# Long convolution: one tile of three as diagonal matmuls, the other two accumulated in PSUM, and row scalings read from PSUM

## Chip, cores and metric

The kernel runs on one core of a Trainium2 chip. The metric is the device time of one execution in microseconds; the time of a kernel is the median of its runs.

## What is computed

A two-block network over 512 positions of width 1024 (batch 1, float32 throughout). The change concerns the first stage of the first block, the three mixers:

```python
a = rmsnorm(h, g_mix)
z = a @ w_in                                    # 1024 -> 2304 columns
za, zb, zc = z[..., :768], z[..., 768:1536], z[..., 1536:]
# A: y = val * sigmoid(gate); causal depthwise convolution of width 31 over 384 channels, + bias;
#    layernorm in groups of 64 channels; silu
ya = conformer_conv(za, conv_a_w, conv_a_b, ln_a_g, ln_a_b)
# B: bg * (causal depthwise convolution of width 3 of cg * xb), 256 channels
yb = short_gated_conv(zb, conv_b_w)
# C: u * (ws @ layernorm(v) + b), a mix over blocks of 128 positions, 384 channels
yc = spatial_gating(zc, ln_c_g, ln_c_b, w_s, b_s)
h = h + concatenate([ya, yb, yc]) @ w_out
```

Behind it come a large expert layer (the product of all 16384 experts, with routing), a gated embedding, and the second block; all of that is left as it is.

## The kernel before

**Layout.** Activations are held transposed: a tile has 128 channels on the partitions and the 512 positions along the free dimension. The 384 channels of the long convolution are three tiles; `conv_a_w` gives each channel 31 weights, which stand as columns in one constant tile (`self.col`).

**Products.** A float32 product is made of three products in the format fp32r: a tensor x is split into `h`, its value cast to that format, and `l = x - h`. `mm3` (L233 to L235) issues h·wh, l·wh and h·wl into one PSUM accumulation. Weights come by DMA into `raw` (SyncE's queue, L202), ScalarE casts them to `wh` (L216), and GpSimd subtracts to get `wl` (L217). Activations are split by `split` (ScalarE, L227; VectorE, L228). `proj` makes one 128x512 output tile from eight such weight units (24 matmuls) in one of four PSUM buffers named `mm`. Two PSUM buffers are named `sm` and two `gg`.

**The stage in program order** (`mix`). The first four column tiles are multiplied while x is still being loaded; `rs` is the reciprocal root mean square of each position, spread over all partitions, and each projection is scaled by it when it leaves PSUM. Then: gate and value of the three tiles of A, which give `yp` (30 zeros and 512 values of y); the first tap of each convolution on ScalarE (L503); the 384 columns of v for C (`vt`), their layernorm; the three `uz` of C; `short(0)`; `short(1)` with `spatial` (48 small matmuls) inside; the remaining 30 taps of each of the three tiles (L590), each one VectorE instruction `ca = yp[:, k : k + 512] * w[k] + ca`; `group_ln` of all three tiles. `group_ln` is a generator: `proj_out` runs one of its steps after each of the eight full-width products of the output projection with the inputs that are ready first (`ys`), and then makes two half-width passes with the late inputs (`late`). At the end of each half the next layer's normalization starts.

**Order.** The order of instructions on each engine is fixed when the program is built. A planner simulates the engines with a cost model and gives each engine, of what is ready in the simulation, what comes first in program order. So the taps, last in program order, fill VectorE's free time. On the chip each engine then works its list in order and waits by semaphores.

**Buffers that matter.** `yq`, the padded input of the short convolution, has one buffer: GpSimd clears its first two columns (L549) for `short(1)` after VectorE has read it for `short(0)` (L555, L557). GpSimd also does the scaling of `g` (L493), of `uz` (L540) and of the six inputs of `short` (L484), the product `yq` (L550), the last product of `short` (L558), and the bias and gate of `spatial` (L576, L577). For these ScalarE first copies the tile out of PSUM.

Of the kernel before, what the change touches and what calls it, by code (L numbers as in the profile page):

```python
# [10 lines left out]
F32 = mybir.dt.float32  # L11
F32R = mybir.dt.float32r
# [4 lines left out]
AF = mybir.ActivationFunctionType  # L17
ALU = mybir.AluOpType
# [4 lines left out]
P = 128  # L23
S = 512
NT = S // P
# [99 lines left out]
def run(gen):  # L125
    for _ in gen:
        pass
# [12 lines left out]
class Net:  # L140
# [166 lines left out]
            self.nc.tensor.matmul(ss[:, t : t + 1], sq[t * P // HS][:, c], self.ones, start=True, stop=True)  # L307
        return ss

    def rsqrt(self, ss, dim, w=NT):  # L310

        ms = self.small(w, tag="ms")
        self.nc.vector.tensor_scalar(ms, ss[:, :w], SQ / dim, SQ * EPS, ALU.mult, ALU.add)
        return self.inv_sqrt(ms, w)

    def inv_sqrt(self, ms, w):

        v = self.nc.vector
        y, a, b = (self.small(w, tag=t, bufs=n) for t, n in (("ry", 4), ("ra", 2), ("rb", 2)))
        yi = y.bitcast(I32)  # L320
        v.tensor_scalar(yi, ms.bitcast(I32), 1, None, ALU.logical_shift_right)
        v.tensor_scalar(yi, yi, -1.0, float(0x5F3759DF), ALU.mult, ALU.add)
        v.tensor_tensor(a, y, y, ALU.mult)
        v.tensor_tensor(a, a, ms, ALU.mult)
        v.scalar_tensor_tensor(b, a, -10.0 / 3, a, ALU.add, ALU.mult)
        v.scalar_tensor_tensor(y, b, 5.0, y, ALU.add, ALU.mult)
        v.tensor_tensor(a, y, y, ALU.mult)
        v.scalar_tensor_tensor(a, a, -0.5 / SQ, ms, ALU.mult, ALU.mult)
        v.scalar_tensor_tensor(y, a, 1.5, y, ALU.add, ALU.mult)
        return y  # L330
# [66 lines left out]
        return xs  # L397


    def group_ln(self, ys, lng, lnb, func, out):  # L400

        nc = self.nc
        blk = self.col("blk", 0, 2)
        w = 2 * NT

        def stats(tiles):
            ss = self.psm()
            for c, y in enumerate(tiles):
                for t in range(NT):
                    o = c * w + 2 * t  # L410
                    nc.tensor.matmul(ss[:, o : o + 2], y[:, t * P : (t + 1) * P], blk, start=True, stop=True)
            return ss

        n = len(ys) * w
        rows = lambda r: [self.heads_rows(r[:, c * w : (c + 1) * w]) for c in range(len(ys))]
        m = self.small(n, tag="lm")
        nc.vector.tensor_scalar(m, stats(ys)[:, :n], 1.0 / 64, None, ALU.mult)
        es = rows(m)
        yield
        yc, q = [], []  # L420
        for c, y in enumerate(ys):
            mb = self.turned(es[c])
            yc.append(self.g(name="yc"))
            nc.vector.tensor_tensor(yc[c], y, mb, ALU.subtract)
            q.append(self.g(name="sq"))
            nc.scalar.activation(q[c], yc[c], AF.Square)
        yield
        yield
        es = rows(self.rsqrt(stats(q), 64, n))
        yield  # L430
        yield
        for c in range(len(ys)):
            rb = self.turned(es[c])
            o = self.g(name="ln")
            nc.vector.scalar_tensor_tensor(o, yc[c], self.col(lng, c), rb, ALU.mult, ALU.mult)
            nc.scalar.activation(o, o, func, bias=self.col(lnb, c))
            out(o)

    def mixers(self, X, then=None):
# [7 lines left out]
    def mix(self, X, mx):  # L447
        nc = self.nc
# [12 lines left out]
        rs = self.e("rs", 1)  # L461
# [4 lines left out]
        bs = mx.tile([P, 3, P], F32, tag="bs", name="bs")  # L466
# [5 lines left out]
        def prod():  # L472
            nonlocal u
            if first:
                return first.pop(0)
            u += KD
            return self.proj(st, u - KD, xs)

        def z(tag, bufs, pool=False):
            p = prod()  # L480
            o = self.e(tag, bufs)
            if pool:
                nc.scalar.copy(o, p)
                nc.gpsimd.tensor_tensor(o, o, rs, ALU.mult)  # L484
            else:
                nc.vector.tensor_tensor(o, p, rs, ALU.mult)
            return o

        yp = []
        for c in range(3):  # L490
            g = z("za", 3)
            nc.scalar.activation(g, g, AF.Sigmoid)
            nc.gpsimd.tensor_tensor(g, g, rs, ALU.mult)  # L493
            y = mx.tile([P, 30 + S], F32, tag="yp", name=self.nm("yp"), bufs=3)
            nc.gpsimd.memset(y[:, :30], 0.0)
            nc.vector.tensor_tensor(y[:, 30:], prod(), g, ALU.mult)
            yp.append(y)
        ya = []
        for c in range(3):
            a = self.e("ca", 3)  # L500
            w = lambda k, c=c: self.col("conv_a_w", 31 * c + k)
            tap = lambda k, c=c: yp[c][:, k : k + S]
            nc.scalar.activation(a, tap(0), AF.Identity, bias=self.col("conv_a_b", c), scale=w(0))  # L503
            ya.append((a, w, tap))
        w1 = self.psm()
        for c in range(3):
            for h in range(2):
# [15 lines left out]
                    self.mm3(vp[t], (xs[k][0][:, sl], xs[k][1][:, sl]), st.unit(u + 3 * k, 3), k == 0, k == KD - 1)  # L523
        u += 3 * KD
        for t, p in enumerate(vp):
            v = mx.tile([P, 384], F32, tag="vt", name=self.nm("vt"), bufs=NT)
            nc.scalar.activation(v, p, AF.Copy, scale=rc[:, t : t + 1])
            m = self.small(6, tag="vm")
            nc.vector.tensor_reduce(m, h6(v), AX.X, ALU.add)
            nc.vector.tensor_scalar(m, m, -1.0 / 64, None, ALU.mult)  # L530
            nc.vector.tensor_tensor(h6(v), h6(v), m[:, :, None].to_broadcast([P, 6, 64]), ALU.add)
            q = self.g(name="sq")
            nc.scalar.activation(q[:, :384], v, AF.Square)
            nc.vector.tensor_reduce(var[:, 6 * t : 6 * t + 6], h6(q[:, :384]), AX.X, ALU.add)
            vt.append(v)
        uz = []
        for c in range(3):
            uz.append(self.e("zu", 3))
            nc.scalar.copy(uz[c], prod())
            nc.gpsimd.tensor_tensor(uz[c], uz[c], rs, ALU.mult)  # L540
        r = self.rsqrt(var, 64, 6 * NT)
        for t in range(NT):
            rb = r[:, 6 * t : 6 * t + 6, None].to_broadcast([P, 6, 64])
            nc.vector.tensor_tensor(h6(vt[t]), h6(vt[t]), rb, ALU.mult)

        def short(c, between=lambda: None):
            cg, xb = z("zb", 4, True), z("zb", 4, True)
            y = mx.tile([P, 2 + S], F32, tag="yq", name=self.nm("yq"), bufs=1)
            nc.gpsimd.memset(y[:, :2], 0.0)  # L549
            nc.gpsimd.tensor_tensor(y[:, 2:], cg, xb, ALU.mult)  # L550
            between()
            bg = z("zb", 4, True)
            a = self.e("cb", 2)
            w = lambda k: self.col("conv_b_w", 3 * c + k)
            nc.vector.tensor_scalar(a, y[:, 0:S], w(0), None, ALU.mult)  # L555
            for k in range(1, 3):
                nc.vector.scalar_tensor_tensor(a, y[:, k : k + S], w(k), a, ALU.mult, ALU.add)  # L557
            nc.gpsimd.tensor_tensor(a, a, bg, ALU.mult)  # L558
            return a

        sg = []
# [1 line left out]
        def spatial():  # L563
            for c in range(3):
                mp = self.psm()
                for h in range(2):
                    for t in range(NT):
                        nc.tensor.matmul(
                            mp[64 * h : 64 * h + 64, t * P : (t + 1) * P],
                            vt[t][:, c * P + 64 * h : c * P + 64 * h + 64], wsT[:, 2 * c + h, :],  # L570
                            start=True, stop=True,
                        )
                o = self.e("sg", 3)
                nc.scalar.activation(o, mp, AF.Copy, scale=self.col("ln_c_g", c))
                o3 = o.rearrange("p (t i) -> p t i", t=NT)
                nc.gpsimd.tensor_tensor(o3, o3, bs[:, c, None, :].to_broadcast([P, NT, P]), ALU.add)  # L576
                nc.gpsimd.tensor_tensor(o, o, uz[c], ALU.mult)  # L577
                sg.append(o)

        free = [(("za", 3), ("za", 3)), (("zu", 3), ("zu", 3)), (("zb", 4), ("zb", 4)), (("zb", 4), ("zb", 4))]  # L580
        late = []
        out = lambda o: late.append(self.split(o, tags=free[len(late)]))
        ys = [self.split(short(0))]
        b1 = short(1, spatial)
        ys += [self.split(o) for o in (sg[0], sg[1], b1)]
        out(sg[2])
        done = []
        for a, w, tap in ya:
            for k in range(1, 31):
                nc.vector.scalar_tensor_tensor(a, tap(k), w(k), a, ALU.mult, ALU.add)  # L590
            done.append(a)
        return ys, late, self.group_ln(done, "ln_a_g", "ln_a_b", AF.Silu, out)


    def peer_norm(self, X):
# [1093 lines left out]
```

## Time and profile before

| what | value |
|---|---|
| median of 3 runs | 3199.23 us (3198.02 to 3207.88) |
| the profiled execution | 3196.37 us, span 3194.6 us, mean granted TensorE clock 0.977 |
| TensorE (PE) busy | 3048.8 us, 95% of the span, 15428 matmuls |
| VectorE (DVE) busy | 1905.5 us, 60% |
| ScalarE (ACT) busy | 1049.6 us, 33% |
| GpSimd (POOL) busy | 1465.6 us, 46% |
| DMA | 424.88 MB, mean 133 GB/s |

The profile is of one execution. Its span runs from the first to the last instruction; the execution is 1.8 us longer. PEld is TensorE's loading of weights, which overlaps its matmuls. Matmuls are pipelined and their ends are modelled, so the distance between the starts of two tells their cost, not the duration shown. The granted clock is given as a share of full speed: 1.0 is 2.4 GHz, 0.5 is 1.2 GHz. A time line gives the start, the duration, the instruction as "out<-in" with tile names, the count where several were merged, and in brackets the idle time before and what ended it.

### The profile page before, as it was taken

How to read it: one execution, taken by the hardware profiler on the slowest of the kernel's cores; microseconds unless marked ns; L12 is line 12 of the kernel's file. 1: busy time of each engine (PE TensorE's matmuls, PEld its weight loads, DVE VectorE, ACT ScalarE, POOL GpSimd, SP SyncE). 2: the span in 40 equal slices, each digit the busy share in tenths (PEclk: the TensorE clock that was granted, in tenths of full speed). 3: DMA queues.
4: the chain of work that ended last, by engine and by line, in shares of the span. 5: the costliest groups of instructions: out<-in, count | busy, mean ns of one | idle time of the engine just before them, and what ended most of it. 6: DMA issues, size and time to landing. Idle time of an engine off the chain costs nothing.

```text
span 3194.6 us, 38906 instructions
## 1 busy us (share of the span) xinstructions
PE 3048.8 (95%) x15428; PEld 2545.1 (80%) x15428; DVE 1905.5 (60%) x3262; ACT 1049.6 (33%) x1632; POOL 1465.6 (46%) x777
## 2 busy tenths in 40 slices
PE   8589999999999999999999988899999999999998
PEld 7478888777878888888888877778888887888887
DVE  8964778988667676676555566666211277552123
ACT  4232222444422322222222344343322234432222
POOL 5635666333345444454444443533444431234454
PEclk9889999999999999999999989999999999999999
DMA  3222333565775656665555311112222221122321
GB/s 135 73 79 93 119 119 139 198 237 208 264 247 197 211 199 207 214 224 193 202 188 177 109 67 60 53 41 79 89 91 105 99 76 38 53 92 76 116 88 65
DMA packets 131926, 424.88 MB, mean 133 GB/s; under 512 B 7824, under 2 KB 73872, under 8 KB 97184
## 3 DMA queue, kind: packets, MB, share of 16 engines
q1 hardware_dynamic: 131744, 422.40, 37.5%
q8 instruction: 121, 1.98, 0.3%
q14 instruction: 61, 0.50, 0.1%
HBM read 367.84 MB, written 54.53 MB: 132 GB/s over the span
## 4 chain that ended last, share of the span: by engine, by line
PE 47%; DVE 5%; issue 1%; ACT 1%; POOL 1%; DVEq 0%; POOLq 0%; ACTq 0%
PE mm L233 15%; PE mm L234 15%; PE mm L235 15%; DVE l L380 1%; PE sm L1239 1%; PE sm L1203 1%; DVE sq L297 0%; DVE m L371 0%; PE gg L1266 0%; PE sm L307 0%; PE gg L1260 0%; DVE x L980 0%; PE mm L1395 0%; PE sm L337 0%; POOL wl L217 0%
## 5 line engine op out<-in xcount | busy, mean ns | idle before, releaser
L217 POOL TENSOR_TENSOR wl<-raw,wh 128x1024 fp32r<-128x1024 f32 (+4 forms) x526 | 1280.2, 2456 | 1544.5 <-ACT wh L216 1537.2
L233 PE MATMUL mm<-h,wh 128*128 128x512 f32 (+1 forms) x2524 | 962.0, 382 | 24.3 <-DVE x L980 7.5
L235 PE MATMUL mm<-h,wl 128*128 128x512 f32 (+1 forms) x2524 | 951.6, 378 | 23.0 <-POOL wl L217 22.9
L234 PE MATMUL mm<-l,wh 128*128 128x512 f32 (+1 forms) x2428 | 924.9, 381 | 16.8 <-DVE l L228 12.4
L216 ACT CAST wh<-raw 128x1024 fp32r<-128x1024 f32 (+4 forms) x526 | 510.1, 996 | 938.1 <-issue 524.1
L235 PEld LDWEIGHTS mm<-h,wl 128*128 128x128 f32 x2524 | 482.0, 191 | 112.7 <-POOL wl L217 26.7
L233 PEld LDWEIGHTS mm<-h,wh 128*128 128x128 f32 x2524 | 482.5, 191 | 111.5 <-DVE x L980 8.7
L234 PEld LDWEIGHTS mm<-l,wh 128*128 128x128 f32 x2428 | 464.6, 191 | 100.6 <-DVE l L228 13.0
L233 PE MATMUL mm<-ah,wh 128*128 128x512 f32 x1024 | 399.3, 390 | 5.3 <-DVE x L640 5.3
L234 PE MATMUL mm<-al,wh 128*128 128x512 f32 x1024 | 399.1, 390 | 0.0
L235 PE MATMUL mm<-ah,wl 128*128 128x512 f32 x1024 | 399.0, 390 | 0.0
L942 DVE CUSTOM_DVE_ANT_0 aw<-aw,c 128x1024 f32<-128x1024 f32 x96 | 199.6, 2081 | 118.0 <-DMA aw<-in_ada_w 94.8
L640 DVE TENSOR_TENSOR x<-x,mm 128x512 f32<-128x512 f32 x256 | 172.6, 681 | 144.5 <-PE mm L235 144.5
L233 PEld LDWEIGHTS mm<-ah,wh 128*128 128x128 f32 x1024 | 192.6, 188 | 46.8 <-DVE x L640 4.4
L234 PEld LDWEIGHTS mm<-al,wh 128*128 128x128 f32 x1024 | 192.5, 188 | 40.1
L235 PEld LDWEIGHTS mm<-ah,wl 128*128 128x128 f32 x1024 | 192.6, 188 | 40.0
L1488 DVE TENSOR_TENSOR sg<-sg,mm 128x512 f32<-128x512 f32 (+1 forms) x48 | 30.9, 643 | 301.4 <-PE mm L235 288.0
L629 ACT CAST ah<-a 128x512 fp32r<-128x512 f32 x128 | 79.4, 621 | 333.8 <-DVE a L627 202.2
L980 DVE SCALAR_TENSOR_TENSOR x<-mm,mod,x 128x256 f32<-128x256 f32 (+1 forms) x112 | 66.5, 595 | 188.5 <-PE mm L235 188.4
L627 DVE TENSOR_TENSOR a<-a,g 128x512 f32<-128x512 f32 x128 | 139.8, 1118 | 61.6 <-DMA a<-act_d 47.4
L630 DVE TENSOR_TENSOR al<-a,ah 128x512 fp32r<-128x512 f32 x128 | 141.2, 1109 | 40.7 <-ACT ah L629 39.5
L233 PE MATMUL mm<-g,wh 128*128 128x512 f32 (+1 forms) x416 | 148.6, 357 | 0.0
(391 smaller groups left out, 3789.4 us busy)
## 6 DMA issues: line engine op xcount, KB each, us to landing
raw<-in_expert_u SPq DMA_DIRECT2D x64, 1024.0 KB, 5.3
raw<-in_expert_v SPq DMA_DIRECT2D x64, 1024.0 KB, 5.1
aw<-in_ada_w SPq DMA_DIRECT2D x96, 512.0 KB, 4.6
raw<-in_ffn_w_in SPq DMA_DIRECT2D x44, 1024.0 KB, 4.8
g_d<-gs SPq DMA_DIRECT2D x16, 2048.0 KB, 7.9
g<-g_d SPq DMA_DIRECT2D x32, 1024.0 KB, 6.3
act_d<-a SPq DMA_DIRECT2D x18, 1024.0 KB, 3.9
a<-act_d SPq DMA_DIRECT2D x18, 1024.0 KB, 4.8
```

What stands on the lines that cost most here:

```text
L216: self.keep(nc.scalar.copy(h[:, c], raw[:, c]))
L217: nc.gpsimd.tensor_tensor(lo[:, c], raw[:, c], h[:, c].bitcast(F32), ALU.subtract)
L233: nc.tensor.matmul(out, w[0], x[0], start=start, stop=False)
L234: nc.tensor.matmul(out, w[0], x[1], start=False, stop=False)
L235: nc.tensor.matmul(out, w[1], x[0], start=False, stop=stop)
L380: nc.vector.scalar_tensor_tensor(lo[:, c], t, sh(k), h[:, c].bitcast(F32), ALU.add, ALU.subtract)
L627: nc.vector.tensor_tensor(v3(a), v3(a), g4[:, :, j, :], ALU.mult)
L629: nc.scalar.copy(h, a)
L630: nc.vector.tensor_tensor(lo, a, h.bitcast(F32), ALU.subtract)
L640: nc.vector.tensor_tensor(X[n], X[n], p, ALU.add)
L942: nc.vector.tensor_tensor_reduce(w, w, c, 1.0, 0.0, ALU.mult, ALU.add, self.mod[:, i : i + 1])
L980: self.nc.vector.scalar_tensor_tensor(x, p, self.mod[:, o + n : o + n + 1], x, ALU.mult, ALU.add)
```

## The change

- Two of the three convolution tiles accumulate their taps in PSUM (`gg`) instead of SBUF; only the last tap writes `ca` in SBUF. Their 60 taps are traced at fixed places between the other work (`tap(n)`), instead of at the end.
- The third tile goes to TensorE: `yp` is split into `yh` and `yl`, the 31 weights into `wh` and `wl`; for each tap ScalarE makes two 128x128 diagonal matrices (`dh`, `dl`: the identity scaled by a column of weights; six buffers each), and `mm3` multiplies them with the shifted `yh`, `yl`, all 31 taps into one PSUM tile. ScalarE adds the bias when it copies it out.
- `group_ln` is called twice: for the first two tiles, its steps between the diagonal products, and for the third, its steps in `proj_out` as before.
- Row scalings (`g`, `uz`, the inputs of `short`) are VectorE instructions that read the projection from PSUM. `cg` is scaled by `rs2`, the square of `rs`, and `xb` is not scaled or stored by itself: `y = xb * cg` reads it from PSUM. `short`'s other products and the two steps of `spatial` are VectorE's too, those of `spatial` reading PSUM. GpSimd keeps the clearing of paddings and the weight splits.
- `spatial` comes after `short(1)`, no longer inside it. The new parameters `room` (the width of a small buffer) and `c0` (the number of the first tile) let `group_ln` work on part of the tiles.

```diff
+    def rsqrt(self, ss, dim, w=NT, room=None):
...
-    def group_ln(self, ys, lng, lnb, func, out):
+    def group_ln(self, ys, c0, lng, lnb, func, out):
...
-        def z(tag, bufs, pool=False):
-            p = prod()
+        def z(tag, bufs, scale=None):
             o = self.e(tag, bufs)
-            if pool:
-                nc.scalar.copy(o, p)
-                nc.gpsimd.tensor_tensor(o, o, rs, ALU.mult)
-            else:
-                nc.vector.tensor_tensor(o, p, rs, ALU.mult)
+            nc.vector.tensor_tensor(o, prod(), rs if scale is None else scale, ALU.mult)
             return o
+        def taps():
+            for c in range(2):
+                acc = self.ps("gg", 2)
+                nc.scalar.activation(acc, tap(0), AF.Identity, bias=self.col("conv_a_b", c), scale=w(0))
+                for k in range(1, 31):
+                    if k == 30:
+                        done.append(self.e("ca", 3))
+                    o = done[c] if k == 30 else acc
+                    nc.vector.scalar_tensor_tensor(o, tap(k), w(k), acc, ALU.mult, ALU.add)
+                    yield
...
+        gated(0)
+        gated(1)
+        nc.vector.tensor_tensor(rs2, rs, rs, ALU.mult)
+        tap(12)
+        gated(2)
+        nc.scalar.copy(yh, yp[2])
+        nc.vector.tensor_tensor(yl, yp[2], yh.bitcast(F32), ALU.subtract)
...
+        def conv_mm():
+            p = self.ps()
+            for k in range(31):
+                dh, dl = (mx.tile([P, P], F32R, tag=t, name=self.nm(t), bufs=6) for t in ("dh", "dl"))
+                nc.scalar.activation(dh, self.ident, AF.Copy, scale=wh.bitcast(F32)[:, k : k + 1])
+                nc.scalar.activation(dl, self.ident, AF.Copy, scale=wl[:, k : k + 1])
+                self.mm3(p, (dh, dl), (yh[:, k : k + S], yl[:, k : k + S]), k == 0, k == 30)
+                yield
+            done.append(self.e("ca", 3))
+            nc.scalar.activation(done[2], p, AF.Identity, bias=self.col("conv_a_b", 2))
...
         for t, p in enumerate(vp):
+            tap(4)
...
-            uz.append(self.e("zu", 3))
-            nc.scalar.copy(uz[c], prod())
-            nc.gpsimd.tensor_tensor(uz[c], uz[c], rs, ALU.mult)
+            uz.append(z("zu", 3))
+            tap(6)
...
-            cg, xb = z("zb", 4, True), z("zb", 4, True)
+            cg = z("zb", 4, rs2)
+            tap(3)
             y = mx.tile([P, 2 + S], F32, tag="yq", name=self.nm("yq"), bufs=1)
             nc.gpsimd.memset(y[:, :2], 0.0)
-            nc.gpsimd.tensor_tensor(y[:, 2:], cg, xb, ALU.mult)
-            between()
-            bg = z("zb", 4, True)
+            nc.vector.tensor_tensor(y[:, 2:], prod(), cg, ALU.mult)
+            tap(3)
+            bg = z("zb", 4)
...
-            nc.gpsimd.tensor_tensor(a, a, bg, ALU.mult)
+            nc.vector.tensor_tensor(a, a, bg, ALU.mult)
+            tap(3)
...
-                nc.scalar.activation(o, mp, AF.Copy, scale=self.col("ln_c_g", c))
-                o3 = o.rearrange("p (t i) -> p t i", t=NT)
-                nc.gpsimd.tensor_tensor(o3, o3, bs[:, c, None, :].to_broadcast([P, NT, P]), ALU.add)
-                nc.gpsimd.tensor_tensor(o, o, uz[c], ALU.mult)
+                nc.vector.scalar_tensor_tensor(
+                    t3(o), t3(mp), self.col("ln_c_g", c), bs[:, c, None, :].to_broadcast([P, NT, P]), ALU.mult, ALU.add
+                )
+                nc.vector.tensor_tensor(o, o, uz[c], ALU.mult)
...
-        b1 = short(1, spatial)
+        b1 = short(1)
+        spatial()
         ys += [self.split(o) for o in (sg[0], sg[1], b1)]
         out(sg[2])
-        done = []
-        for a, w, tap in ya:
-            for k in range(1, 31):
-                nc.vector.scalar_tensor_tensor(a, tap(k), w(k), a, ALU.mult, ALU.add)
-            done.append(a)
-        return ys, late, self.group_ln(done, "ln_a_g", "ln_a_b", AF.Silu, out)
+        run(conv)
+        ln = self.group_ln(done[:2], 0, "ln_a_g", "ln_a_b", AF.Silu, out)
+        for k, _ in enumerate(conv_mm()):
+            if k % 4 == 3:
+                next(ln, None)
+        run(ln)
+        return ys, late, self.group_ln(done[2:], 2, "ln_a_g", "ln_a_b", AF.Silu, out)
```

## Rows read from the trace of the kernel before

**Rows 1.** TensorE's time line, end of the stage: start us, us, instruction.

```profile
199.97 0.28 PE L233 MATMUL mm<-za,wh 128*128 128x256 f32 x1
```

**Rows 2.** Windows: length, then busy us (instructions) of PE, PEld, DVE, ACT, POOL; PEclk; DMA.

```profile
33.40:107.10 73.70, 69.20 (x321) 59.38 (x317) 71.57 (x82) 25.73 (x46) 50.02 (x30) 0.98 0.26 87
107.10:127.80 20.70, 2.56 (x13) 1.79 (x11) 20.66 (x32) 0.00 (x0) 1.73 (x3) 0.67 0.00 0
127.80:149.60 21.80, 16.52 (x86) 12.85 (x86) 21.31 (x13) 5.81 (x9) 21.64 (x12) 0.85 0.28 97
149.60:162.00 12.40, 0.04 (x2) 0.04 (x1) 12.26 (x10) 3.66 (x6) 9.93 (x6) 0.58 0.00 0
162.00:175.30 13.30, 11.85 (x40) 10.17 (x41) 8.82 (x11) 0.62 (x1) 4.36 (x2) 0.50 0.22 79
175.30:201.20 25.90, 25.90 (x137) 21.95 (x136) 16.30 (x30) 10.01 (x14) 4.78 (x3) 0.93 0.12 41
```

**Rows 3.** Waits of TensorE, 0 to 250 us: total us, times, longest.

```profile
PE mm L235 <- POOL wl L217: 18.1, 1, 18.1
PE mm L234 <- DVE l L228: 12.4, 1, 12.4
PE mm L233 <- DVE yp L496: 3.8, 1, 3.8
PE mm L233 <- ACT h L227: 2.7, 1, 2.7
PE sm L568 <- ACT sg L574: 2.6, 1, 2.6
PE sm L411 <- DVE ca L590: 1.5, 1, 1.5
```

**Rows 4.** GpSimd's time line; in brackets its idle time before and what ended it.

```profile
126.03 0.10 POOL L549 MEMSET yq<- 128x2 f32 x1 [21.83 <-DVE cb L557]
126.17 1.52 POOL L217 TENSOR_TENSOR wl<-raw,wh 128x512 fp32r<-128x512 f32 x1
```

**Rows 5.** VectorE's time line, taps (L590) and a reader of yq (L557).

```profile
108.22 14.65 DVE L590 SCALAR_TENSOR_TENSOR ca<-yp,cols,ca 128x512 f32<-128x512 f32 x22
125.18 0.74 DVE L557 SCALAR_TENSOR_TENSOR cb<-yq,cols,cb 128x512 f32<-128x512 f32 x1
134.91 21.52 DVE L590 SCALAR_TENSOR_TENSOR ca<-yp,cols,ca 128x512 f32<-128x512 f32 x12
167.54 1.52 DVE L590 SCALAR_TENSOR_TENSOR ca<-yp,cols,ca 128x512 f32<-128x512 f32 x2
```

**Rows 6.** Groups by line and shape, 0 to 250 us: count, busy us, mean ns, idle before.

```profile
L590 DVE SCALAR_TENSOR_TENSOR ca<-yp,cols,ca 128x512 f32<-128x512 f32 x90 | 97.8, 1124 | 0.6
L435 DVE SCALAR_TENSOR_TENSOR ln<-yc,cols,gg 128x512 f32<-128x512 f32 x3 | 2.1, 742 | 0.1
L486 DVE TENSOR_TENSOR za<-mm,rs 128x512 f32<-128x512 f32 x3 | 2.0, 684 | 1.4 <-ACT rs L462 1.4
```

**Rows 7.** VectorE's time line just after 200 us.

```profile
203.01 0.42 DVE L441 TENSOR_TENSOR x<-x,mm 128x256 f32<-128x256 f32 x1 [1.00 <-PE mm L235]
203.92 2.23 DVE L297 TENSOR_TENSOR sq<-sq,sq 128x256 f32<-128x256 f32 x1 [0.48 <-ACT sq L291]
```

**Rows 8.** GpSimd's time line just after 200 us.

```profile
201.11 4.75 POOL L217 TENSOR_TENSOR wl<-raw,wh 128x1024 fp32r<-128x1024 f32 x2 [11.95 <-ACT wh L216]
```

**Rows 9.** TensorE's time line, first and last of twenty matmuls issued at full clock.

```profile
104.92 0.39 PE L233 MATMUL mm<-h,wh 128*128 128x512 f32 x1
109.23 0.39 PE L234 MATMUL mm<-l,wh 128*128 128x512 f32 x1
```

**Rows 10.** Groups by line and shape, whole span, ScalarE.

```profile
L385 ACT ACTIVATE h<-x,cols 128x512 fp32r<-128x512 f32 x12 | 8.5, 722 | 7.2 <-DVE x L640 5.5 <-DMA x<-in_xT 1.6
L1401 ACT ACTIVATE pe<-mm,mx 128x512 f32<-128x512 f32 x8 | 5.5, 690 | 9.3 <-DVE mx L1399 9.3
L1401 ACT ACTIVATE pe<-mm,mx 128x128 f32<-128x128 f32 x8 | 2.9, 368 | 9.8 <-DVE mx L1399 5.6 <-PE sm L1418 3.6 <-PE gg L234 0.6
```

More of the change, by code (lines that the diff above doesn't have):

```diff
@@ L308, in sums, with inv_sqrt @@
         return ss
-    def rsqrt(self, ss, dim, w=NT):
-        ms = self.small(w, tag="ms")
+    def rsqrt(self, ss, dim, w=NT, room=None):
+        ms = self.small(room or w, tag="ms")[:, :w]
         self.nc.vector.tensor_scalar(ms, ss[:, :w], SQ / dim, SQ * EPS, ALU.mult, ALU.add)
-        return self.inv_sqrt(ms, w)
-    def inv_sqrt(self, ms, w):
+        return self.inv_sqrt(ms, w, room)
+    def inv_sqrt(self, ms, w, room=None):
         v = self.nc.vector
-        y, a, b = (self.small(w, tag=t, bufs=n) for t, n in (("ry", 4), ("ra", 2), ("rb", 2)))
+        y, a, b = (self.small(room or w, tag=t, bufs=n)[:, :w] for t, n in (("ry", 4), ("ra", 2), ("rb", 2)))
         yi = y.bitcast(I32)
@@ L415, in group_ln @@
         rows = lambda r: [self.heads_rows(r[:, c * w : (c + 1) * w]) for c in range(len(ys))]
-        m = self.small(n, tag="lm")
+        m = self.small(3 * w, tag="lm")[:, :n]
         nc.vector.tensor_scalar(m, stats(ys)[:, :n], 1.0 / 64, None, ALU.mult)
@@ L428, in group_ln @@
         yield
-        es = rows(self.rsqrt(stats(q), 64, n))
+        es = rows(self.rsqrt(stats(q), 64, n, 3 * w))
         yield
@@ L434, in group_ln @@
             o = self.g(name="ln")
-            nc.vector.scalar_tensor_tensor(o, yc[c], self.col(lng, c), rb, ALU.mult, ALU.mult)
-            nc.scalar.activation(o, o, func, bias=self.col(lnb, c))
+            nc.vector.scalar_tensor_tensor(o, yc[c], self.col(lng, c0 + c), rb, ALU.mult, ALU.mult)
+            nc.scalar.activation(o, o, func, bias=self.col(lnb, c0 + c))
             out(o)
@@ L477, in prod, with tap, gated @@
             return self.proj(st, u - KD, xs)
-        def z(tag, bufs, pool=False):
-            p = prod()
+        def z(tag, bufs, scale=None):
             o = self.e(tag, bufs)
-            if pool:
-                nc.scalar.copy(o, p)
-                nc.gpsimd.tensor_tensor(o, o, rs, ALU.mult)
-            else:
-                nc.vector.tensor_tensor(o, p, rs, ALU.mult)
-            return o
-        yp = []
-        for c in range(3):
+            nc.vector.tensor_tensor(o, prod(), rs if scale is None else scale, ALU.mult)
+            return o
+        def taps():
+            for c in range(2):
+                acc = self.ps("gg", 2)
+                w = lambda k: self.col("conv_a_w", 31 * c + k)
+                tap = lambda k: yp[c][:, k : k + S]
+                nc.scalar.activation(acc, tap(0), AF.Identity, bias=self.col("conv_a_b", c), scale=w(0))
[5 more added lines that the diff above has]
+                    yield
+        yp, done = [], []
+        conv = taps()
+        def tap(n):
+            for _ in range(n):
+                next(conv, None)
+        def gated(c):
             g = z("za", 3)
             nc.scalar.activation(g, g, AF.Sigmoid)
-            nc.gpsimd.tensor_tensor(g, g, rs, ALU.mult)
+            nc.vector.tensor_tensor(g, g, rs, ALU.mult)
             y = mx.tile([P, 30 + S], F32, tag="yp", name=self.nm("yp"), bufs=3)
@@ L497, in mix @@
             yp.append(y)
[L498 to L504, printed above, removed]
+        gated(0)
+        gated(1)
+        rs2 = self.e("rs2", 1)
+        nc.vector.tensor_tensor(rs2, rs, rs, ALU.mult)
+        tap(12)
+        gated(2)
+        yh, yl = (mx.tile([P, 30 + S], F32R, tag=t, name=t) for t in ("yh", "yl"))
+        nc.scalar.copy(yh, yp[2])
+        nc.vector.tensor_tensor(yl, yp[2], yh.bitcast(F32), ALU.subtract)
+        wc = self.col("conv_a_w", 62, 31)
+        wh, wl = (mx.tile([P, 31], dt, tag=t, name=t) for t, dt in (("wch", F32R), ("wcl", F32)))
+        self.tc.keep_in_program_order(nc.scalar.copy(wh, wc))
+        nc.vector.tensor_tensor(wl, wc, wh.bitcast(F32), ALU.subtract)
+        def conv_mm():
[8 more added lines that the diff above has]
+            nc.scalar.activation(done[2], p, AF.Identity, bias=self.col("conv_a_b", 2))
         w1 = self.psm()
@@ L544, in mix, with short @@
             nc.vector.tensor_tensor(h6(vt[t]), h6(vt[t]), rb, ALU.mult)
-        def short(c, between=lambda: None):
-            cg, xb = z("zb", 4, True), z("zb", 4, True)
+        def short(c):
+            cg = z("zb", 4, rs2)
+            tap(3)
             y = mx.tile([P, 2 + S], F32, tag="yq", name=self.nm("yq"), bufs=1)
             nc.gpsimd.memset(y[:, :2], 0.0)
-            nc.gpsimd.tensor_tensor(y[:, 2:], cg, xb, ALU.mult)
-            between()
-            bg = z("zb", 4, True)
+            nc.vector.tensor_tensor(y[:, 2:], prod(), cg, ALU.mult)
+            tap(3)
+            bg = z("zb", 4)
             a = self.e("cb", 2)
@@ L573, in spatial @@
                 o = self.e("sg", 3)
-                nc.scalar.activation(o, mp, AF.Copy, scale=self.col("ln_c_g", c))
-                o3 = o.rearrange("p (t i) -> p t i", t=NT)
-                nc.gpsimd.tensor_tensor(o3, o3, bs[:, c, None, :].to_broadcast([P, NT, P]), ALU.add)
-                nc.gpsimd.tensor_tensor(o, o, uz[c], ALU.mult)
+                t3 = lambda a: a.rearrange("p (t i) -> p t i", t=NT)
+                nc.vector.scalar_tensor_tensor(
+                    t3(o), t3(mp), self.col("ln_c_g", c), bs[:, c, None, :].to_broadcast([P, NT, P]), ALU.mult, ALU.add
+                )
+                nc.vector.tensor_tensor(o, o, uz[c], ALU.mult)
                 sg.append(o)
```

## The prediction

> **What bounds the kernel now.** I read the page's shares first (the table above): TensorE is busy nearly throughout, so a change can pay only where it idles or runs at a reduced clock. Then I cut the opening stage (the mixers, which end where the first half-width product of the output projection issues, at 199.97 us [rows 1]) into stretches with the view of windows [rows 2]. The reader is to see three things there. From 33.4 to 107.1 us TensorE is busy 69.2 of 73.7 us. From 107.1 to 162.0 us it is busy 19.1 of 54.9 us, while VectorE is busy in all but 0.7 us. From 162.0 to 175.3 us TensorE works, but at a granted clock of 0.50. The view of waits names what TensorE waited for [rows 3]: 18.1 us for a `wl` of GpSimd, 12.4 us for an `l` of VectorE, and 2.7, 2.6 and 1.5 us around them.
>
> The time lines say why [rows 4, 5]. GpSimd's queue stands for 21.83 us at the clearing of the second `yq` (L549), because VectorE has not yet read the first one (L557 at 125.18); `yq` has one buffer. The next `wl` is queued behind that memset, and it is what TensorE lacks. VectorE is late because of the taps: 90 of them cost 97.8 us, a mean of 1124 ns [rows 6]. While GpSimd is idle, 22 in a row take 14.65 us, that is 666 ns each; while GpSimd multiplies, 12 take 21.52 us, 1.79 us each [rows 5]. So TensorE waits on VectorE, VectorE is slowed by GpSimd, and GpSimd waits on VectorE.
>
> **The change part by part.** *Taps.* 30 of the 90 taps leave VectorE. The other 60 accumulate in PSUM, so one tensor input is left in SBUF. No row shows VectorE writing PSUM. Two rows show it reading PSUM while GpSimd works: a 128x256 sum with one PSUM input takes 0.42 us, and 0.9 us later the like with both inputs in SBUF takes 2.23 us, both beside a GpSimd subtraction of 4.75 us for two [rows 7, 8]. The same form as a tap (two multiplies, a column pointer, one PSUM input) takes 742 ns at 128x512 [rows 6]. I take 0.74 us, since that row is nearest; the bounds are 0.667 us (a tap with GpSimd idle) and 1.79 us (a tap beside GpSimd, if PSUM spared nothing). 60 x 0.74 = 44.4 us, where 90 cost 97.8.
>
> *Row scalings and products.* Three `g`, three `uz`, six for `short`'s inputs (four, as `xb` is folded into `y`, plus two `y`), two last products, six in `spatial`, `rs2` and `yl` are 22 instructions on VectorE at 0.68 us (the row of `za` with a PSUM input [rows 6]): 15.0 us more. GpSimd loses as many, ScalarE its copies out of PSUM. Ten of the 22 have both inputs in SBUF; if each met a GpSimd instruction it would take 1.8 instead of 0.67, 11 us in all.
>
> VectorE is busy 125.8 us from 33.4 to 162.0 (the four rows from 33.4 on [rows 2]). 87 taps with 94.5 of the 97.8 us fall there (three, 3.3 us, come later), so 31.3 us is other work. New: 31.3 + 15.0 + 44.4 = 90.7 us, so both convolution sums on VectorE are ready at 33.4 + 90.7 = 124 us, or 135 with all of the ten contended.
>
> *The third tile on TensorE.* 31 taps of three products are 93 matmuls of 512 columns. At full clock twenty of them issue from 104.92 to 109.23, 0.227 us apart [rows 9]. That adds 93 x 0.227 = 21.1 us of TensorE work, and no engine hides it: it has to fit into time in which TensorE idles now. Their 62 diagonals are ScalarE instructions of 128x128 with a pointer scale, a form that the trace lacks. The nearest rows are 368 ns (128x128, pointer bias) and 690 ns (128x512, same line), so 0.84 ns a column; from SBUF 512 columns take 722, which makes 0.40 us for 128 [rows 10]. The lower end is 0.30: 0.37 less the 0.07 by which taps in a row overlap on VectorE (0.74 against 0.666). I take 0.37, 22.9 us in all, between 18.6 and 24.8. Twelve can be built ahead, 4.4 us, so the diagonals alone do not set the pace. ScalarE's other work in the stretch of the projection is 10.01 of 25.9 us [rows 2], some 8 us in 21; with it ScalarE could add up to 24.8 + 8 - 4.4 - 21.1 = 7.3 us. I take 2.
>
> The page "ScalarE: Activation LUTs" of the Trainium skill (section "What ACT_TABLE_LOAD costs") gives an ACTIVATE with a pointer operand 280 ns + 0.833 ns a column, 93 ns of it overlapped back to back: 387 ns, or 294, for 128 columns. The trace agrees with its 368. By the page the diagonals would take an estimated 18.2 to 24.0 us; at the lower end the 2 us above would be nothing and the time 3174.
>
> *What TensorE gets back.* The waits at `wl`, `l`, `h`, `sg` and `ca` end if VectorE and GpSimd are no longer late: 18.1 + 12.4 + 2.7 + 2.6 + 1.5 = 37.3 us [rows 3]. The 3.8 us at `yp` I leave in place: there the 4 buffers of `mm` are full, and the taps still run ahead of it. Without the long idle stretches the clock should not fall: from 162.0 to 175.3 it was 0.50 over 11.85 us busy, 5.9 us lost; from 127.8 to 149.6 0.85 over 16.52, 2.5 us lost [rows 2]. Together 45.7 us.
>
> *Order.* What is late next? From 107.1 to the start of the projection at 149.6 TensorE was busy 2.56 + 16.52 us, 2.5 of them lost to the clock [rows 2]; without the waits these 16.6 us end at 124, and the 93 products at 145. VectorE is ready at 124 to 135, so the normalization of two tiles finds its place inside these 21 us, and that of the third inside the eight products of the output projection (96 x 0.227 = 21.8 us), as all three do now. TensorE then decides the end. Nothing is moved past a DMA queue; the weight loads keep their order.
>
> **The sum.** 45.7 - 21.1 - 2 = 22.6 us less. A second count: from 162.0 to 199.97 TensorE spent 38.0 us, of which 21.8 are the 96 products, 5.9 the lost clock and 1.5 a wait, so some 9 are the small normalization products. 145 + 21.8 + 9 puts the first half-width product at 176 instead of 199.97, 24 less. All later work (2994.6 us) moves ahead unchanged. The profiled execution took 3196.4 us, of which 3194.6 is the span: 3173.8. The median of the runs, 3199.2, lies 2.9 above it, so about 3176. With the 3.8 us gained too and no pacing by ScalarE 28.4 us less (3171); with 7.3 of pacing and 2 at the spatial tiles' two PSUM buffers 15.3 less (3184).
>
> **Rivals.** *1. The memset of `yq` still stalls the queue.* The memset, its single buffer and the `wl` behind it stay as they are, and VectorE still works from 33.4 to 124 us with hardly a pause, with the moved scalings ahead of `short`. For it: VectorE ran 22 taps between GpSimd's product and its first reader [rows 5], an order fixed beforehand. Against it: VectorE's delay is mostly contention (1124 against 666 ns), and that goes. If half of the 18.1 us stays, with another 4 us of `sg` and `l`, the gain is 22.6 - 13 = 9.6 us: about 3190.
>
> The Trainium skill speaks for this rival: "SBUF — State Buffer" (section "Who interferes with whom") says that a VectorE instruction with two SBUF inputs contends with a GpSimd one that reads SBUF, and ten of the moved ones are such. The trace agrees [rows 7]: 2.23 us against 0.42.
>
> *2. ScalarE paces the products.* Its queue is in order; a diagonal that waits for a buffer stands ahead of casts and splits. For it: 0.37 x 2 per tap is above TensorE's 0.68. Against: ScalarE is busy only 35.2 of the 128.6 us from 33.4 to 162.0 [rows 2] and loses copies. A stall of 10 us leaves a gain of about 12: 3187.
>
> *3. Slower: the taps in PSUM are long.* Each needs the sum before it, and the write into PSUM is unpriced. With t us a tap, the sums are ready at 33.4 + 46.3 + 60t; two tiles' normalization takes some 12 us, and then come 25 of the projection with the third's: 116.7 + 60t. That equals 199.97 at t = 1.39; at 1.79 it is 224, 24 us slower (3223). Against: a dependent pair in SBUF took 1.52 us for two, the last two taps [rows 5], so waiting for the result adds little.
>
> *4. More is gained.* The planner can put the 93 products into the gaps before 107 too: about 3166.
>
> **How the numbers follow.** Likeliest (own range 3171 to 3184) 0.52; rival 1 0.22; rival 2 0.09; rival 3 0.08; rival 4 0.09. The range runs from 3167 to 3191: it takes in the likeliest, most of rivals 1 and 2 and half of 4. A measurement tells 0.3%, 9.6 us, from no change. Faster: 0.52 + 0.09 + 0.08 (rival 2) + 0.15 (most of 1) = 0.84. Same: 0.07 of rival 1, 0.01 of 2 and 0.02 of 3, 0.10. Slower: 0.06.
>
> **What would show it.** Right: taps near 0.74 us at any activity of GpSimd; no wait of TensorE for `wl` over 3 us from 100 us on; granted clock near 1.00 from 107 us to the projection; 93 products in under 24 us; the first half-width product at 172 to 182 us. Wrong: L549's successor waiting over 9 us (rival 1); TensorE waiting for `dh` or `dl` (rival 2); taps over 1 us (rival 3).

## The result and the profile after

The kernel after takes 3166.19 us (median of 4 runs, 3165.51 to 3166.90), the kernel before 3198.68 on the same chip: a ratio of 0.9900 (0.9888 to 0.9913), faster by some 32 us, where 22.6 had been forecast; the time lies just under the forecast range of 3167 to 3191. The profiled execution took 3166.64 us, its span is 3164.8 us at a mean granted clock of 0.986.

TensorE's time line puts the first half-width product, which was at 199.97 [rows 1], here:

```profile
168.49 0.28 PE L233 MATMUL mm<-za,wh 128*128 128x256 f32 x1
```

The view of windows from 34 us to that product and from there to the end, for the kernel after (columns as in [rows 2]):

```profile
34.28:168.49 134.21, 132.83 (x669) 113.13 (x670) 105.43 (x176) 57.91 (x124) 47.20 (x31) 1.00 0.22 77
168.49:3164.80 2996.31, 2896.50 (x14733) 2416.70 (x14731) 1741.69 (x3052) 984.71 (x1521) 1356.96 (x702) 0.99 0.38 136
```

The same view of the kernel before, and the five stretches in which its clock was at 0.50 (1.2 GHz) while TensorE had work:

```profile
34.22:199.97 165.75, 124.62 (x577) 104.94 (x578) 149.48 (x172) 43.82 (x72) 92.37 (x53) 0.85 0.18 62
199.97:3194.60 2994.63, 2896.92 (x14733) 2418.26 (x14731) 1733.88 (x3052) 984.54 (x1521) 1354.87 (x702) 0.98 0.39 136
...
55.96:59.44 3.48, 3.48 (x13) 3.48 (x12) 3.48 (x7) 0.39 (x2) 0.00 (x0) 0.51 0.35 120
127.75:131.05 3.30, 3.30 (x8) 2.62 (x9) 3.23 (x3) 0.00 (x0) 3.30 (x3) 0.50 0.01 2
137.90:141.41 3.51, 3.51 (x13) 2.70 (x11) 3.47 (x2) 0.00 (x0) 3.51 (x2) 0.52 0.22 93
161.96:175.62 13.66, 12.20 (x41) 10.48 (x42) 8.86 (x11) 0.62 (x1) 4.36 (x2) 0.51 0.22 77
185.70:189.05 3.35, 3.35 (x11) 2.77 (x11) 2.62 (x3) 0.94 (x1) 3.35 (x2) 0.50 0.00 0
```

The stage is 165.75 - 134.21 = 31.5 us shorter, and everything behind it 1.7 longer: 29.8 us of span. The 31.5 divide as follows. TensorE's idle time went from 165.75 - 124.62 = 41.1 us to 1.4. The clock had cost 0.49 x 3.48 + 0.50 x 3.30 + 0.48 x 3.51 + 0.49 x 12.20 + 0.50 x 3.35 = 12.7 us and now costs nothing. TensorE's work at full clock rose from 124.62 - 12.7 = 111.9 to 132.8, by 20.9 us: by the distances of their starts the 93 new products take some 22 us, and the other work some 1 us less. 41.1 - 1.4 + 12.7 - 20.9 = 31.5. The old idle time is exactly the sum of [rows 3]: 18.1 + 12.4 + 3.8 + 2.7 + 2.6 + 1.5.

Three of the five falls stand behind waits (3.8, 18.1 and 12.4 us) and one among the 48 small matmuls of `spatial` with a wait of 2.6 us. The last does not follow a wait. TensorE was busy throughout and had just run 24 matmuls of 128x2; behind them the products issue 0.43 us apart instead of 0.23, as its time line in the kernel before shows:

```profile
183.33 2.99 PE L411 MATMUL sm<-cols,sq 128*128 128x2 f32 x24
...
187.18 0.63 PE L235 MATMUL mm<-h,wl 128*128 128x512 f32 x1
187.61 0.63 PE L233 MATMUL mm<-h,wh 128*128 128x512 f32 x1
```

In the kernel after, the same 24 come as 16 and 8, with other products between, and the clock stays at 1.00; no run here tests whether the division does it.

TensorE's waits in the kernel after, 0 to 220 us; of those longer than 0.6 us only the last shown lies between 34.28 and 168.49:

```profile
PE mm L233 <- ACT wh L216: 5.8, 1, 5.8
PE sm L307 <- DVE sq L297: 4.4, 1, 4.4
...
PE sm L337 <- DVE ry L329: 1.6, 1, 1.6
PE gg L353 <- DVE sh L345: 1.4, 1, 1.4
```

The groups by line and shape, 0 to 220 us, with the new operations:

```profile
L496 DVE SCALAR_TENSOR_TENSOR gg<-yp,cols,gg 128x512 f32<-128x512 f32 x58 | 41.7, 746 | 0.4 <-ACT gg L491 0.3
L534 ACT ACTIVATE dh<-ident,wch 128x128 fp32r<-128x128 f32 x31 | 11.7, 393 | 3.3 <-PE mm L234 3.1
L535 ACT ACTIVATE dl<-ident,wcl 128x128 fp32r<-128x128 f32 x31 | 11.6, 388 | 1.1 <-DVE wcl L527 0.8 <-PE mm L235 0.3
L616 DVE TENSOR_TENSOR sg<-sg,zu 128x512 f32<-128x512 f32 x3 | 4.5, 1530 | 0.0
```

A tap takes 746 ns, beside GpSimd and apart from it. The time lines show it beside GpSimd's subtractions from 97.28 us on:

```profile
97.28 4.24 POOL L217 TENSOR_TENSOR wl<-raw,wh 128x512 fp32r<-128x512 f32 x3
```

```profile
98.29 0.74 DVE L496 SCALAR_TENSOR_TENSOR gg<-yp,cols,gg 128x512 f32<-128x512 f32 x1
98.94 1.42 DVE L595 TENSOR_TENSOR cb<-cb,zb 128x512 f32<-128x512 f32 x1
100.29 0.74 DVE L496 SCALAR_TENSOR_TENSOR gg<-yp,cols,gg 128x512 f32<-128x512 f32 x1
```

Between two taps of 0.74 us stands a product of the same size with both inputs in SBUF, and it takes 1.42. That is the difference that the taps escaped (12 in a row took 1.79 us each, [rows 5]). "SBUF — State Buffer" of the Trainium skill (section "Who interferes with whom") names this condition, two SBUF inputs beside a GpSimd instruction that reads SBUF; these rows agree with it.

The second sum is ready at 104.8 us, not at 124 to 135, and the value of the third tile leaves PSUM at 45.68 instead of 54.72 us. VectorE's time lines for that value, after, then before:

```profile
45.68 0.68 DVE L512 TENSOR_TENSOR yp<-mm,za 128x512 f32<-128x512 f32 x1
```

```profile
54.72 0.68 DVE L496 TENSOR_TENSOR yp<-mm,za 128x512 f32<-128x512 f32 x1
```

The products run from 113.55 to 142.74, with other small products between them. TensorE's time line shows two of one diagonal, 0.23 us apart:

```profile
125.68 0.39 PE L233 MATMUL mm<-yh,dh 128*128 128x512 f32 x1
125.91 0.39 PE L234 MATMUL mm<-yl,dh 128*128 128x512 f32 x1
```

### The profile page after: what moved, and what is told of

Its sections match the earlier page's. It is cut to its first block, busy times and chain, and to the rows that moved or that the text cites. A ratio compares the mean times of both kernels' runs of the same rounds, so it can differ in the third digit from the quotient of the medians.

```text
span 3164.8 us, 39156 instructions
## 1 busy us (share of the span) xinstructions
PE 3055.7 (97%) x15521; PEld 2551.1 (81%) x15521; DVE 1870.4 (59%) x3266; ACT 1063.8 (34%) x1684; POOL 1422.5 (45%) x755
## 4 chain that ended last, share of the span: by engine, by line
PE 47%; DVE 5%; ACT 1%; issue 1%; POOL 1%; DMA 0%; DVEq 0%; POOLq 0%; SPq 0%; ACTq 0%
PE mm L233 15%; PE mm L234 15%; PE mm L235 15%; DVE l L380 1%; PE sm L1244 1%; PE sm L1280 1%; DVE sq L297 0%; DVE m L371 0%; PE gg L1307 0%; PE sm L307 0%; PE gg L1301 0%; DVE x L1021 0%; PE mm L1436 0%; POOL wl L217 0%; POOL kl L1231 0%
## 5 line engine op out<-in xcount | busy, mean ns | idle before, releaser
L983 DVE CUSTOM_DVE_ANT_0 aw<-aw,c 128x1024 f32<-128x1024 f32 x96 | 206.8, 2156 | 108.0 <-DMA aw<-in_ada_w 85.4
```

The source lines that it names most:

```text
L983: nc.vector.tensor_tensor_reduce(w, w, c, 1.0, 0.0, ALU.mult, ALU.add, self.mod[:, i : i + 1])
```

## The experiments

The ratio is to the kernel before on the same chip. "Last sum" is when VectorE adds the last of the 16 half-width products of the output projection to x: 227.40 us before, 195.91 after. What follows it took 2963 to 2974 us in the profiled executions, with no order by kernel, so the last sum shows the stage by itself. It is of one execution: in the full change repeated it is at 199.19, since TensorE's clock was at 0.50 there from 34 to 41 us, which cost 3.1 us.

| kernel | us | ratio (95%) | last sum |
|---|---|---|---|
| full change | 3166.19 | 0.9900 (0.9888 to 0.9913) | 195.91 |
| before + taps in PSUM | 3161.97 | 0.9884 (0.9868 to 0.9901) | 191.86 |
| before + scalings | 3193.94 | 0.9991 (0.9981 to 1.0000) | 217.74 |
| before + diagonals | 3201.24 | 1.0012 (1.0003 to 1.0022) | 230.43 |
| before + second `yq` | 3198.98 | 1.0004 (0.9993 to 1.0014) | 227.21 |
| after, taps in SBUF | 3179.43 | 0.9942 (0.9925 to 0.9958) | 210.43 |
| after, scalings back | 3183.99 | 0.9964 (0.9951 to 0.9976) | 212.68 |
| after, no diagonals | 3167.91 | 0.9907 (0.9890 to 0.9923) | 197.20 |
| after, `yl` products left out | 3158.24 | 0.9875 (0.9858 to 0.9891) | 189.59 |
| 16 taps on TensorE | 3155.95 | 0.9869 (0.9852 to 0.9885) | 188.25 |
| 8 taps on TensorE | 3153.74 | 0.9857 (0.9839 to 0.9874) | 187.76 |

### One part alone

**Taps in PSUM.**

```diff
-            a = self.e("ca", 3)
+            a = self.ps("gg", 2)
...
-                nc.vector.scalar_tensor_tensor(a, tap(k), w(k), a, ALU.mult, ALU.add)
+                o = self.e("ca", 3) if k == 30 else a
+                nc.vector.scalar_tensor_tensor(o, tap(k), w(k), a, ALU.mult, ALU.add)
```

> The kernel before with one part of the change: the taps of all three tiles accumulate in PSUM, still 90 on VectorE and last in program order. Theory (VectorE's queue, lengthened by GpSimd, made TensorE wait): 90 taps take 60 to 67 us instead of 97.8, the wait for wl behind the memset of yq and the wait for l shrink, 20 to 30 us less, about 3174. Rival (GpSimd's part of the circle keeps it closed): under 9.6 us less.

It gained 34.6 us, more than the theory had given it. The taps in its groups by line, TensorE's waits for `wl` from 34 us on, and the windows of its stage:

```profile
L595 DVE SCALAR_TENSOR_TENSOR gg<-yp,cols,gg 128x512 f32<-128x512 f32 x87 | 61.9, 750 | 0.7
```

```profile
PE mm L235 <- POOL wl L217: 1.5, 2, 1.3
```

```profile
34.30:164.42 130.12, 120.42 (x576) 100.41 (x577) 112.00 (x172) 43.62 (x72) 75.21 (x53) 0.93 0.24 80
...
125.00:145.00 20.00, 16.31 (x57) 13.12 (x58) 14.95 (x19) 4.23 (x6) 10.63 (x7) 0.66 0.15 52
```

GpSimd still does all its scalings (75.2 us busy), and still no wait for `wl` from 34 us on is longer than 1.3 us. TensorE is idle for 130.1 - 120.4 = 9.7 us, and its clock, with a mean of 0.66 from 125 to 145, costs it 7.7 us in the stage; but it has no 93 products to do. Each kernel is planned anew, so its order differs a little too: here 11 taps run ahead of the value of the third tile, 12 in the kernel before. No run separates the order from the price of a tap. Against the full change on one chip:

> The kernel before with the taps of all three tiles accumulated in PSUM and nothing else, beside the full change on the same chip. If the whole gain is the price of a tap, it is at least as fast as the full change: 3160 to 3164, against 3165 to 3167.

> The full change, on the same chip as the kernel with the taps in PSUM alone. 3165 to 3167 as before; if the difference of 4 us between the two was one of chips, they are equal here.

The taps alone took 3159.92 us (3157.47 to 3164.16), the full change 3168.34 (3167.43 to 3171.06): the ranges do not meet. Of the change as a whole, this one part carries the gain; the other two together gave some back.

**Scalings on VectorE.** `z`, `uz`, `short` and `spatial` as in the change; taps in SBUF, no diagonals, the old order.

> The kernel before with one part of the change: row scalings, products of the short convolution and steps of the spatial mix on VectorE, reading PSUM; 90 taps on VectorE in SBUF. Theory: VectorE gets 15 us more and its taps lose part of the contention (a mean of 0.8 to 0.95 us instead of 1.12, 16 to 29 us less), so it is early by 0 to 14 us: 3185 to 3199. Rival (GpSimd's queue was the limit): 25 us less or more.

It is about as fast as before, inside the range of the theory, but its taps, at 1048 ns, are dearer than the 0.8 to 0.95 us that the theory went by. The profiled execution is the fastest of its ten runs, 6 us below their median, so its waits and its last sum flatter the kernel. The wait for `wl` shrinks from 18.1 to 7.2, but VectorE, with 15 us more to do, is late for `spatial`:

```profile
PE sm L562 <- DVE sg L569: 14.5, 1, 14.5
PE mm L235 <- POOL wl L217: 7.8, 2, 7.2
```

**Third tile as diagonals.** `conv_mm` and the divided `group_ln`; 60 taps in SBUF.

> The kernel before with one part of the change: the third tile as diagonal products on TensorE, the other two in SBUF on VectorE as before. Theory: VectorE loses 30 taps of 1.12 us, 34 us, TensorE gets 21.1: between 5 and 20 us less, 3179 to 3194. Rival (TensorE's added work is not hidden): no change or slower.

4 us slower, as the rival had it. The taps that stay take 1037 ns, and the stalls remain:

```profile
PE mm L235 <- POOL wl L217: 13.8, 1, 13.8
PE mm L233 <- ACT dh L519: 4.7, 1, 4.7
PE gg L353 <- DVE sh L345: 4.3, 2, 3.0
PE mm L233 <- DVE yp L497: 3.8, 1, 3.8
```

**A second `yq`.**

```diff
-            y = mx.tile([P, 2 + S], F32, tag="yq", name=self.nm("yq"), bufs=1)
+            y = mx.tile([P, 2 + S], F32, tag="yq", name=self.nm("yq"), bufs=2)
```

> The kernel before with a second buffer for yq, so that GpSimd's clearing of it waits for nothing. Theory (VectorE is the limit, the memset only passes its lateness on): the 18.1 us wait of TensorE for wl goes, and TensorE waits as much longer for the splits behind it: at most 5 us less. Rival (the memset is the cause by itself): 15 to 18 us less.

No difference, as the theory had it. The 18.1 us at `wl` are gone, and 20.7 us stand at `spatial` instead:

```profile
PE sm L568 <- ACT sg L574: 20.7, 1, 20.7
PE mm L234 <- DVE l L228: 14.4, 1, 14.4
```

So the memset of [rows 4] only handed on VectorE's lateness.

### One part undone

**Taps back in SBUF.**

```diff
-                acc = self.ps("gg", 2)
+                acc = self.e("cacc", 2)
```

> The changed kernel with the two tiles' taps accumulated in SBUF again. Theory (TensorE sets the end, VectorE has some 20 us to spare): taps beside GpSimd take 1.8 us again, the mean is 0.9 to 1.1 us, the two sums are ready 12 to 25 us later than 104.8, and the time is 3166 to 3173. Rival (ending the contention of the taps with GpSimd is the gain): about 20 us slower, 3186.

13 us slower than the full change; neither expectation held. With GpSimd freed of 22 products a tap in SBUF costs 975 ns, 229 more than in PSUM; 60 of them make 13.7 us of VectorE's time. Of the 14.5 us by which the stage is longer, TensorE idles 9.0 (7.6 of its waits are for `wl`), and its clock costs 4.6:

```profile
PE mm L235 <- POOL wl L217: 7.6, 3, 5.6
```

```profile
L496 DVE SCALAR_TENSOR_TENSOR cacc<-yp,cols,cacc 128x512 f32<-128x512 f32 x58 | 54.8, 975 | 0.4 <-ACT cacc L491 0.4
```

**Scalings back on ScalarE and GpSimd.**

> The changed kernel with the row scalings, the products of the short convolution and the two steps of the spatial mix back on ScalarE and GpSimd. Theory (GpSimd's 35 us more lie beside TensorE's work, since taps in PSUM don't slow it or are slowed by it): 3166 to 3174, with a few short waits of TensorE for wl. Rival (the circle VectorE, GpSimd, TensorE has to be cut at GpSimd): 12 us slower or more, with a wait for wl behind the memset of yq of over 9 us.

About 18 us slower than the full change: more than the theory, of the rival's size, but not in its way, since the wait for `wl` is 0.7 us. The taps still take 747 ns and VectorE has time to spare; it is GpSimd's chain `yq`, `cb`, `sg` that ends late. ScalarE, in order, waits for `sg` with a split, and the diagonals are queued behind it. ScalarE's time line, then TensorE's:

```profile
127.73 0.62 ACT L227 CAST h<-sg 128x512 fp32r<-128x512 f32 x1 [9.39 <-POOL sg L620]
128.25 0.40 ACT L537 ACTIVATE dh<-ident,wch 128x128 fp32r<-128x128 f32 x1
```

```profile
128.71 0.75 PE L233 MATMUL mm<-yh,dh 128*128 128x512 f32 x1 [5.17 <-ACT dh L537]
137.74 1.97 PE L353 MATMUL gg<-ident,sh 128*128 128x128 f32 x8 [5.35 <-DVE sh L345]
```

TensorE waits for `dh`, the sign of rival 2, but the other way round: a split that waits for GpSimd stands ahead of the diagonals. With the diagonals alone the 4.7 us at `dh` have the same form. In the full change the scalings on VectorE are what keeps this away.

**No diagonals.** All three tiles' taps on VectorE in PSUM, one `group_ln` of three tiles at the end.

> The changed kernel with the third tile's taps on VectorE too (accumulated in PSUM like the other two) and no diagonal products. Theory (since the change TensorE's own work sets the end of the stage, and VectorE has room after 105 us): 93 products fewer are 21.1 us less of TensorE work, 30 taps more are about 20 us more of VectorE work, the three sums are ready at 138 to 145 us and the first half-width product comes at 152 to 160 instead of 168.5: a median of 3150 to 3158. Rival (taking the third tile off VectorE is what pays): slower than 3166 by 9 us or more.

Neither: 3167.91, as the full change. TensorE has 21 us less to do and none of it comes out. The last tap of the third tile is at 150.04 (at 140.27 with the taps alone in PSUM, where the scalings are not on VectorE), the normalization of all three follows it, and TensorE has only the projection left to cover that. Its first half-width products, those whose inputs were ready, come at 148.34, ahead of the forecast, but the last sum comes 1.3 us after that of the full change. Its waits, and a window:

```profile
PE gg L353 <- DVE sh L345: 5.3, 2, 2.8
PE sm L586 <- DVE sg L593: 3.5, 1, 3.5
```

```profile
145.00:170.00 25.00, 17.82 (x87) 15.74 (x86) 16.50 (x33) 7.97 (x11) 4.65 (x2) 0.66 0.21 78
```

Idle for 7.2 of 25 us, at a mean clock of 0.66, which costs 5.9 us more. So in the full change the products do useful work as cover, but they cost as much as they cover.

### What the products cost

The third product of each tap (`yl` x `dh`) is left out, so the third tile's convolution loses its correction term:

> The changed kernel with two of the three products per tap of the third tile: the one of yl with dh is left out of the computation; both diagonals are still built. Theory (TensorE sets the end): 31 matmuls of 0.227 us less, 7.0 us, so 3159. Rival (ScalarE paces the diagonal products): 62 diagonals and its other work still take some 26 us, so the time stays within 2 us of 3166.

8 us faster (its last sum 6.3 us earlier) for 31 x 0.232 = 7.2 us less work, as the theory said: in the kernel after, TensorE's work sets the time of the stage. That led to a division of the tile:

```diff
-            for c in range(2):
+            for c in range(3):
+                k0 = 16 if c == 2 else 0
...
-            for k in range(31):
+            for k in range(16):
...
-            nc.scalar.activation(done[2], p, AF.Identity, bias=self.col("conv_a_b", 2))
+            nc.vector.tensor_tensor(done[2], p, done[2], ALU.add)
```

> The kernel after, with the third tile's 31 taps divided: 16 on TensorE (48 products instead of 93), 15 on VectorE in PSUM, and one VectorE sum that joins the two parts. Theory: in the kernel after TensorE has no idle time left in the stage, so each tap that it loses gives back its 0.68 us: 15 x 0.68 = 10.2 us, as leaving out the 31 products with yl gave about 8 for 7; VectorE's 15 more instructions (11 us) end near 116 us, still ahead of the normalization. Time 3155 to 3159, first half-width sum near 160. Rival: the products also cover the normalization of the tiles, as the kernel without diagonals showed; with half of them VectorE's later sums leave TensorE waiting at L353 or for ca, and the time stays at 3163 to 3168.

> As the kernel with divided taps, with 8 on TensorE (24 products) and 23 on VectorE. Theory: 23 x 0.68 = 15.6 us less on TensorE, but VectorE's sums end near 122 us, when TensorE has little left ahead of the projection: waits of 3 to 6 us come back, time 3153 to 3160. Rival: as without diagonals, 3164 to 3169.

Both came out as the theory had it. They are faster than the full change on their chip (3168.34), by 12.4 and 14.6 us; the medians are also below the 3159.92 of the taps in PSUM alone, by 4.0 and 6.2, though the runs with 8 taps overlap with its runs. The windows of the kernel with 16 taps:

```profile
34.30:160.80 126.50, 123.74 (x624) 105.57 (x625) 110.85 (x191) 48.57 (x94) 48.44 (x31) 0.99 0.24 82
...
125.00:145.00 20.00, 20.00 (x111) 17.05 (x110) 11.89 (x30) 8.10 (x16) 0.00 (x0) 1.00 0.00 1
```

TensorE stays busy in the stretch in which the taps alone left it idle and slow, with half the products. With 8 taps on TensorE, in the slowest of its four runs, which is the profiled one, 2.8 us of wait at L353 are back and the clock has a mean of 0.86 from 145 to 170 us; the runs of the two overlap (3153.03 to 3157.07 and 3150.14 to 3161.25), so which is better stays open.

## Why the prediction was right and wrong

**Right:** the mechanism. TensorE's stalls came from VectorE's contended taps; in PSUM a tap takes 0.746 us (0.74 forecast); no wait for `wl` is left; the clock is 1.00; VectorE's sums are early; TensorE sets the end. The experiments bear out the chain: the taps' place moves the time, the memset does not.

**Wrong:** the size, 22.6 us instead of 31.5 in the stage, so the first half-width product comes at 168.49 and not at 172 to 182. The step that failed is "what TensorE gets back", with 45.7 us where 41.1 - 1.4 + 12.7 = 52.4 came back; the 2 us set against it for ScalarE were not needed either:

- *The wait at `yp`* (3.8 us) was left in place, "there the 4 buffers of `mm` are full, and the taps still run ahead of it". They do, 8 of them where 12 did, but with fewer and cheaper taps the value leaves PSUM 9 us earlier, before TensorE needs the buffer. The wait went as well with the taps alone in PSUM, with the scalings alone, and with the taps back in SBUF; it stayed with the diagonals alone and with the second `yq`. It was a wait on VectorE like the others, and belonged in the sum.
- *The clock* was read from two stretches, 8.4 us; five falls make 12.7. The two that were missed (at 55.96 and at 185.70) are 3.4 us; most of the rest was lost in the mean of 0.85 from 127.8 to 149.6, which stands for two falls to 0.50 and an idle stretch at full clock. The 0.93 of [rows 2] from 175.3 on is likewise one short fall, and it came without the idle stretch that the prediction held to be its condition.
- *ScalarE's pacing*, 2 us: none in the full change. A diagonal takes 388 to 393 ns, but in a row they issue 0.295 us apart, two in 0.59 us against TensorE's 0.70, as ScalarE's time line shows below. "ScalarE: Activation LUTs" of the Trainium skill (section "What ACT_TABLE_LOAD costs") gives by its formula an estimated 387 ns for 128 columns, or 294 in a row; these rows agree with it, and the lower of its two sums was the right one.
- Against these stand 1.4 us of a new wait for `sh`. The 93 products were priced at 21.1 us, and the work rose by 20.9.

```profile
125.70 0.39 ACT L534 ACTIVATE dh<-ident,wch 128x128 fp32r<-128x128 f32 x1
125.99 0.39 ACT L535 ACTIVATE dl<-ident,wcl 128x128 fp32r<-128x128 f32 x1
126.28 0.39 ACT L534 ACTIVATE dh<-ident,wch 128x128 fp32r<-128x128 f32 x1
```

22.6 + 3.8 + 4.3 + 2 + 0.2 - 1.4 = 31.5. Behind the stage 1.7 us were lost, a difference that repeats of one kernel also show (4.7 us there between the two profiled executions of the taps in PSUM alone); and the 2.9 us by which the median before exceeded its profiled execution were added and did not come (3166.64 against 3166.19).

**Rivals.** 1: the memset still waits, 6.2 us (97.16), but nothing waits for it; the experiment with a second buffer shows that the stall was not the memset's. 2: TensorE waits for `dh` not in the full change, but with the scalings back and with the diagonals alone, where ScalarE waits for GpSimd. 3: a tap is at 0.746, far from 1.39. 4 gave the time (3166) by luck and not the way: the first product is at 113.55, none fell into the gaps before 107 us; there were no gaps left.

**What the prediction did not ask** is which part pays. It charged the 93 products against the stalls of the whole change; the taps in PSUM alone take TensorE's idle time from 41.1 to 9.7 us and the clock's cost from 12.7 to 7.7, without the charge.

## What to carry to other kernels

Where a vector engine's accumulation slows down beside GpSimd, move the accumulator to PSUM first, and measure that alone before work is moved to TensorE. When several stalls hang on one late engine, add up all of them, the small ones too. Read the lost clock from windows cut where the clock changes: the mean over a longer stretch hides a short fall, and idle time at full clock in it makes the fall look cheaper than it is. Work moved to an engine that sets the time pays only as far as it fills that engine's idle time: divide it so that it does just that.

## What the runs showed of the hardware that was not expected

A tiny VectorE instruction can stand as long as a whole GpSimd instruction. In the kernel after, two 128x8 integer instructions of the reciprocal root take 2.39 and 2.31 us, where the same lines take 0.17 for 128x16 at another place; GpSimd's two subtractions beside them take 4.75 us in all. VectorE's time line, then GpSimd's:

```profile
155.81 2.39 DVE L321 TENSOR_SCALAR ry<-ms 128x8 int32<-128x8 int32 x1
158.23 2.31 DVE L322 TENSOR_SCALAR ry<-ry 128x8 int32<-128x8 int32 x1
160.57 0.17 DVE L323 TENSOR_TENSOR ra<-ry 128x8 f32<-128x8 f32 x1
```

```profile
155.76 4.75 POOL L217 TENSOR_TENSOR wl<-raw,wh 128x1024 fp32r<-128x1024 f32 x2 [38.15 <-ACT wh L216]
```

Each seems to wait for one subtraction to end; no experiment here tested it. They belong to the chain that leads to `sh`, and TensorE's new wait of 1.4 us stands behind it. Such an instruction accumulates nothing, so accumulating in PSUM does not reach it.
